# The start of the first layer reordered, and half PSUM banks for the projection steps beside attention

## The chip, the cores and the metric

The kernel runs on one core of a Trainium2 chip. The metric is device microseconds of one execution; three executions of the kernel before took 1530.9 to 1532.79 us, with a median of 1532.69 us. The engines are named as the profile names them: PE is TensorE (PEld its weight loads), DVE is VectorE, ACT is ScalarE, POOL is GpSimd, SP is SyncE, which issues every DMA of this kernel.

## The reference, cut to what matters

Two layers run one after the other on x (1024 tokens by 1024 features, float32). Each layer is

```
h = rms_norm(x, pre_norm)                       # rows of x times 1/rms, times a gain
proj = h @ w_in                                 # 1024 x 3072: q, k, v and gates of all heads
dq, dk = rotary(dq), rotary(dk)                 # differential attention, 6 heads x 2 maps
gq, gk = rotary(rms_norm(gq)), rotary(rms_norm(gk))   # grouped-query attention, 6 q / 2 kv heads
mk, mv = split(rms_norm(mem) @ w_mem_kv)        # cross attention into 256 memory tokens, 4 heads
o = softmax(q k^T) v  for each head, times silu(gate)
x = x + rms_norm(concat(o) @ w_out, post_norm)
```

Every product is done in split precision: an operand is kept as a rounded "hi" part and the rest as "lo", and three matmuls (hi by hi, hi by lo, lo by hi) stand for one.

## The kernel before, in words

**The planner.** No order is written out by hand. `Plan` runs all the work as small processes against a model of the engines. A process asks for an engine with a priority (a lower number goes first) and an assumed duration; when the model starts the job, its instructions are emitted. The order of emission is the program order of each engine and is fixed from then on. The tile framework under it then adds semaphores wherever two accesses to one tile have to be ordered, by that order. The planner knows only its own events and buffers, not these semaphores.

**The PSUM banks.** PSUM has eight banks. The planner's `Banks` (L145) hands out two tiles of two banks (`pp`, size 2) and four tiles of one bank of 512 columns (`ps`, size 1). `KINDS` (L83) gives each kind of use a priority, the most it may hold, and a size: `st` (projection steps beside attention) up to four, `mx` (row maxima of scores) four, `tr` (transposes) two, `pv` (probabilities times v) one, `s0` and `s1` (projection steps before attention) two each. All of these take from the same four `ps` tiles.

**A projection step** is one chunk of 256 columns of `w_in` for one tile of 128 tokens: 24 matmuls (L518) in four groups of six, a group for each quarter of the weights, all accumulating into 256 columns of a `ps` tile. So a step uses half of the bank that it holds. When its last group is done, `post` (L752) is started for it and `steps` (L807) goes straight on to the next step, which asks for its own slot. `post` empties the bank. For a gate chunk ACT reads it (tanh, L724) and then DVE reads it (L732). For q and k chunks ACT squares it (L676, only heads with a norm) and DVE does three rotary operations on it (L657 twice, once in place, and L659). For v parts ACT (L640) and DVE (L641) read it, and a plain copy is ACT's (L774). Then the slot is freed (`free_ps`). These reads have the priority `POST` of -1 on ACT and DVE; the matmuls of `st` steps have the last priority on PE.

**The stages of a layer.** First `steps` runs the chunks dq0 and dk0 (kinds s0 and s1), then dv0 and the memory's mk and mv. Then attention begins: the d items (12 score maps), later the g and m items. Beside it run the nine chunks of `REST` for eight token tiles, 72 steps of the kind `st`, four of the nine chunks being gates. After attention comes the output projection (L1444), whose tail also normalises and transposes x for the second layer.

**The first layer's begin** is `start_up` (L1752). One matmul group broadcasts the gain vector `pre_norm` over the partitions into a `pp` tile (L1786). Eight x tiles are loaded (five buffers, `XT`). `one(t)` takes each of them through `norm_T` (L489): ACT squares and sums (L491), POOL makes the inverse root (L454, L455), DVE multiplies by it and the gain (L501). Then `split_T` does, twice, four transposes on PE (L476), the hi copy on ACT (L480) and the lo difference on DVE (L481). The same DVE rotates the dq0 and dk0 steps meanwhile. `gm0` (L446) takes the greatest gain on DVE; the scale of v needs it. `weights` (L562) loads four pieces of each chunk through three `rt` buffers, splits them (L410, L411, L412) into eight `wt` slots and goes on to the next chunk when two pieces are ready. The rotary tables of the second kind are loaded and multiplied on POOL (L624, L626).

Of the kernel before, what the change touches and what calls it, by code (L numbers as in the profile page):

```python
# [12 lines left out]
F32 = mybir.dt.float32  # L13
# [9 lines left out]
P = 128  # L23
# [7 lines left out]
NC = 256  # L31
# [22 lines left out]
FIRST = ("dq0", "dk0", "dv0", "mk", "mv")  # L54
# [13 lines left out]
ALT0, ALT1, ALTM = (), (), ()  # L68
# [5 lines left out]
LAT = {"pe": 0.231, "act": 0.176, "dve": 0.165, "pool": 0.121, "hwdge": 0.65, "dma": 0.95}  # L74
DVE_FIX = 0.15
PV_N = 2
XT = 5
DMA_RATE = 300.0

CLOCK_WINDOW, CLOCK_LOW, CLOCK_HIGH = 3.41, 0.33, 0.85  # L80
SLACK = 0.8

KINDS = {'un': (0.5, 2, 2), 'z': (1, 2, 2), 's0': (2, 2, 1), 's1': (0, 2, 1), 'st': (1, 4, 1), 'pv': (1, 1, 1), 'tr': (-1, 2, 1), 'mx': (2, 4, 1), 'zh': (3, 2, 1)}  # L83


def raw(t):
# [3 lines left out]
class Event:  # L90
    def __init__(self, n=1):
        self.n = n
        self.waiters = []
# [51 lines left out]
class Banks:  # L145


    def __init__(self, tiles, kinds):
        self.free_tiles = tiles
        self.kinds = kinds  # L150
        self.held = {k: 0 for k in kinds}
        self.waiters = []
        self.seq = 0
# [6 lines left out]
    def grant(self, plan):  # L160
        rest = []
        while self.waiters:
            w = heapq.heappop(self.waiters)
            _, limit, size = self.kinds[w[3]]
            if self.held[w[3]] < limit and self.free_tiles[size]:
                self.held[w[3]] += 1
                plan.push(plan.t, w[2], (w[3], size, None, self.free_tiles[size].pop(0)))
            else:
                rest.append(w)
        for w in rest:  # L170
            heapq.heappush(self.waiters, w)

    def free(self, plan, slot):
        kind, size, _, t = slot
        self.free_tiles[size].append(t)
        self.held[kind] -= 1
        self.grant(plan)

# [109 lines left out]
def trunk(ctx, tc, t_in, t_out):  # L288
    nc = tc.nc
    act, dve, pool, pe = nc.scalar, nc.vector, nc.gpsimd, nc.tensor  # L290
    pl = Plan()
# [10 lines left out]
    big = ctx.enter_context(tc.tile_pool(name="big", bufs=16))  # L302
    psp = ctx.enter_context(tc.tile_pool(name="psum", bufs=1, space=PSUM))
    banks = Banks({2: [psp.tile([P, D], F32, name=f"pp{i}") for i in range(2)],
                   1: [psp.tile([P, 512], F32, name=f"ps{i}") for i in range(4)]}, KINDS)
    R = {"rt": Ring(RT_BUFS), "wt": Ring(W_SLOTS), "big": Ring(16)}

    def open_pool(name, bufs=1, side=None):
# [10 lines left out]
    def wait(ev):  # L319
        return "wait", ev  # L320
# [13 lines left out]
    def DVE(n, fn, prio=0, ops=1, fast=False, port=False):  # L334

        return use("dve", DVE_FIX * ops + n / (1900.0 if fast else 960.0), fn, prio, None, port)
# [126 lines left out]
    def free_ps(slot):  # L463
        banks.free(pl, slot)

    def split_T(src, hi, lo, halves=(0, 1), prio=0):

        done = Event(len(halves))

        def half(h):  # L470
            slot = yield take_ps("tr")
            ps = slot[3]

            def f():
                for j in range(4):
                    pe.transpose(out=ps[:, j * P:(j + 1) * P], in_=src(4 * h + j), identity=ident)  # L476

            yield PE(1024, f, prio)
            v = ps[:, 0:512].rearrange("p (b t) -> p b t", t=P)
            yield ACT(512, lambda: act.activation(hi[:, 4 * h:4 * h + 4, :], v, AF.Copy), prio, "p")  # L480
            yield DVE(512, lambda: dve.tensor_sub(out=lo[:, 4 * h:4 * h + 4, :], in0=v,  # L481
                                                  in1=raw(hi)[:, 4 * h:4 * h + 4, :]), prio)
            free_ps(slot)

        for h in halves:
            pl.spawn(half(h), done)
        yield wait(done)

    def norm_T(xt, gbc, hn, hi, lo, ev=None, alt=False):  # L489
        ss = small.tile([P, 1], F32, name="ss")  # L490
        yield ACT(1024, lambda: act.activation(hi.rearrange("p a b -> p (a b)"), xt, AF.Square, accum_out=ss))  # L491
        box = []
        yield from rstd_of(ss, 1, 1.0 / D, box, -2)
        if ev is not None:
            yield wait(ev)
            gbc = gbc[0]
        if alt:
            yield ACT(1024, lambda: act.activation(hn, xt, AF.Copy, scale=box[0][:, 0:1]))
            yield POOL(1024, lambda: pool.tensor_mul(out=hn, in0=hn, in1=gbc))
        else:  # L500
            yield DVE(1024, lambda: dve.scalar_tensor_tensor(out=hn, in0=xt, scalar=box[0][:, 0:1], in1=gbc,  # L501
                                                             op0=ALU.mult, op1=ALU.mult), port=ev is None)
        yield from split_T(lambda b: hn[:, b * P:(b + 1) * P], hi, lo)

    def new_big():
        return big.tile([P, S], F32R, name="big")
# [30 lines left out]
    def make_layer(l):  # L537
        L = Layer()
# [22 lines left out]

        def weights(chunks):  # L562
            for c in chunks:
                src = t_in["w_mem_kv"][l] if c in ("mk", "mv") else w_in
                vmax = None
                if c in VCOLS:
                    vmax = small.tile([P, 8], F32, name="gm")
                    pl.spawn(vscale(vmax, (lambda: mgm[0]) if c == "mv" else (lambda: L.gmx), L.W[c], sc, VKEY[c]))
                evs = []
                for j in range(4):  # L570
                    ev = Event()
                    pl.spawn(load_piece(src, j, CHUNKS[c], L.W[c], c, vmax, {FIRST[0]: -7, FIRST[1]: -5}.get(c, 0),
                                        L.rt.pop(0) if L.rt else None), ev)
                    evs.append(ev)
                if c != FIRST[0]:
                    yield wait(evs[1])
# [230 lines left out]
        def steps(chunks, kind, prio):  # L807

            todo = []
            for c in chunks:  # L810
                todo += [(c, t) for t in range(2 if c in ("mk", "mv") else NT)]
            yield wait(opened)
            for c, t in todo:
                n = 2 if c in ("mk", "mv") else NT
                if c in ("mk", "mv"):
                    yield wait(mem_ready[t])
                    hi, lo = mT[t]
                else:
                    yield wait(L.xT_ev[t])
                    hi, lo = L.xT[t]  # L820
                yield wait(L.W[c]["ev"][0])
                nat = None
                if c in scr:
                    ni = yield take("nat")
                    nat = (Q["pj"].tile([P, NC], F32, name="nat", bufs=NAT), ni)
                slot = yield take_ps(kind)
                ps = slot[3][:, 0:NC]
                yield from matmul_chunk(ps, hi, lo, L.W[c], t == n - 1, prio)
                if c == REST[-1]:
                    if t == 0:  # L830
                        rest_on.fire(pl)
                    for s in L.xT_slot[t]:
                        free("big", s)
                if c == "mv" and t == 1:
                    close_pool(pools["mp"])
                    open_attn()
                pl.spawn(post(c, t, slot, ps, nat), pend)
# [914 lines left out]
    def start_up():  # L1752
# [26 lines left out]
        def gain0():  # L1779

            slot = yield take_ps("z")
            ps = slot[3]

            def f():
                for h in range(2):
                    pe.matmul(ps[:, h * 512:(h + 1) * 512], lhsT=on[0:1, 0:P], rhs=grow[0:1, h * 512:(h + 1) * 512],  # L1786
                              start=True, stop=True)

            yield PE(8200, f)
            gbc.append(ps)  # L1790
            gain_ev.fire(pl)
            yield wait(L.xT_ev[1])
            yield DVE(1024, gm0, 2)
            for e in L.xT_ev:
                yield wait(e)
            free_ps(slot)

        def loads():
            g = dmas([(grow, t_in["pre_norm"][0:1], 4)], -10)
            yield "until", pl.t + 0.01  # L1800
            pl.spawn(load_x(0, evs[0], -9))
            pl.spawn(L.begin())
            yield wait(g)
            yield wait(on_ev)
            pl.spawn(gain0())
            pl.spawn(load_x(1, evs[1], -6))
            pl.spawn(dma(lin, t_in["lin_tab"], 128, -4))
            for t in range(2, NT):
                pl.spawn(load_x(t, evs[t], -3))
# [18 lines left out]
        def one(t):  # L1828
            yield wait(evs[t])
            b0 = yield take("big")  # L1830
            h = new_big()
            b1 = yield take("big")
            o = new_big()
            hi, lo = (x.rearrange("p (k t) -> p k t", t=P) for x in (h, o))
            L.xT[t] = (hi, lo)
            L.xT_slot[t] = (b0, b1)
            xt, i = xts[t]
            yield from norm_T(xt, gbc, xt, hi, lo, gain_ev, t in ALT0)
            free("xt", i)
            L.xT_ev[t].fire(pl)  # L1840

# [54 lines left out]
```

## Time and profile before

| | |
|---|---|
| median of three executions | 1532.69 us |
| the profiled execution's own time | 1529.82 us |
| its span | 1528.0 us |
| granted PE clock, mean over the span | 0.994 |
| PE busy | 1474.7 us (97%) |
| DVE, POOL, ACT busy | 1016.4, 907.6, 893.2 us |

The span runs from the first to the last instruction; the time has 1.8 us more around it. "Busy" is the time in which an engine had an instruction running. Matmuls overlap one another, so a busy PE can still be slower than its peak. In a row of the windows, the figure after an engine is its busy time in that stretch with the number of instructions, and PEclk is the granted share of the PE clock (0.50 is the lower of its two levels, 1.2 GHz instead of 2.4). In a row of the timeline the bracket says how long the engine had been idle before and what ended it.

### The profile page before, as it was taken

How to read it: one execution, taken by the hardware profiler on the slowest of the kernel's cores; microseconds unless marked ns; L12 is line 12 of the kernel's file. 1: busy time of each engine (PE TensorE's matmuls, PEld its weight loads, DVE VectorE, ACT ScalarE, POOL GpSimd, SP SyncE). 2: the span in 40 equal slices, each digit the busy share in tenths (PEclk: the TensorE clock that was granted, in tenths of full speed). 3: DMA queues.
4: the chain of work that ended last, by engine and by line, in shares of the span. 5: the costliest groups of instructions: out<-in, count | busy, mean ns of one | idle time of the engine just before them, and what ended most of it. 6: DMA issues, size and time to landing. Idle time of an engine off the chain costs nothing.

```text
span 1528.0 us, 39224 instructions
## 1 busy us (share of the span) xinstructions
PE 1474.7 (97%) x15920; PEld 1366.0 (89%) x15920; DVE 1016.4 (67%) x1886; ACT 893.2 (58%) x1429; POOL 907.6 (59%) x654
## 2 busy tenths in 40 slices
PE   6999999999999999999999999999999999999997
PEld 5999999999999988887889999999999998888886
DVE  6646676777864797844566386767877748887233
ACT  5232748677668486683333347578667756686511
POOL 5033848789778495571142348469897767685400
PEclk9999999999999999999999999999999999999999
DMA  6335322233232643215255433133342246422242
GB/s 221 107 115 153 85 81 81 85 105 99 77 94 80 170 123 92 72 57 183 97 170 159 124 103 104 42 102 94 102 118 60 65 121 192 113 68 71 95 138 97
DMA packets 166658, 164.75 MB, mean 108 GB/s; under 512 B 14924, under 2 KB 140588, under 8 KB 166477
## 3 DMA queue, kind: packets, MB, share of 16 engines
q1 hardware_dynamic: 166477, 162.25, 36.3%
q8 instruction: 125, 2.05, 0.6%
q14 instruction: 56, 0.46, 0.1%
HBM read 111.74 MB, written 50.09 MB: 106 GB/s over the span
## 4 chain that ended last, share of the span: by engine, by line
PE 81%; issue 6%; DVE 5%; DMA 3%; POOL 3%; ACT 1%; SPq 1%; POOLq 0%; DVEq 0%; ACTq 0%
PE ps L518 33%; PE pp L1444 9%; PE ps L1067 6%; PE pp L1077 6%; PE ps L529 4%; PE ps L531 4%; PE ps L530 4%; PE ps L1279 3%; PE ps L1280 2%; PE pp L1291 2%; PE pp L1292 2%; DVE mx L938 1%; PE ps L476 1%; PE ps L1444 1%; POOL el L901 1%
## 5 line engine op out<-in xcount | busy, mean ns | idle before, releaser
L901 POOL TENSOR_TENSOR el<-e,eh 128x1024 f16<-128x1024 f32 x254 | 563.4, 2231 | 169.2 <-ACT eh L898 161.1
L518 PE MATMUL ps<-wt,big 128*128 128x256 f32 x4608 | 642.4, 286 | 14.4 <-DVE sl L712 3.7
L518 PEld LDWEIGHTS ps<-wt,big 128*128 128x128 f32 x4608 | 605.9, 191 | 34.9 <-DVE sl L712 4.3
L938 DVE TENSOR_REDUCE mx<-ps 128x1 f32<-128x512 f32 (+1 forms) x608 | 404.2, 684 | 118.1 <-PE ps L1067 81.2
L894 ACT ACTIVATE e<-pp 128x1024 f32<-128x1024 f32 x304 | 308.9, 1023 | 99.5 <-PE pp L1077 52.2
L898 ACT ACTIVATE eh<-e 128x1024 f16<-128x1024 f32 x264 | 277.5, 1058 | 2.9
L529 PEld LDWEIGHTS <-eh 128*128 128x128 f16 x2144 | 194.8, 96 | 13.6 <-issue 9.0
L531 PEld LDWEIGHTS <-el 128*128 128x128 f16 x2144 | 196.5, 99 | 4.7 <-POOL el L901 4.2
L530 PEld LDWEIGHTS <-eh 128*128 128x128 f16 x2144 | 196.7, 97 | 0.9 <-issue 0.8
L412 POOL TENSOR_TENSOR wt<-rt,wt 128x512 fp32r<-128x512 f32 x84 | 122.4, 1469 | 123.8 <-ACT wt L410 87.0
L454 POOL TENSOR_SCALAR u<-ss 128x1 f32<-128x1 f32 (+3 forms) x95 | 23.6, 249 | 238.2 <-DVE ss L1585 96.2
L1067 PE MATMUL ps<-sdk,sdq 96*128 96x512 f32 x384 | 159.1, 414 | 0.8 <-DVE gs L732 0.8
L529 PE MATMUL ps<-vd,eh 128*128 128x65 f16 x1536 | 151.3, 193 | 0.0
L530 PE MATMUL ps<-vd,eh 128*128 128x64 f16 x1536 | 150.4, 194 | 0.0
L531 PE MATMUL ps<-vd,el 128*128 128x65 f16 x1536 | 149.9, 192 | 0.0
L1077 PE MATMUL pp<-sdq,sdk 98*128 98x256 f32 x768 | 125.3, 285 | 0.5 <-DMA sdq<-nl 0.5
L1077 PEld LDWEIGHTS pp<-sdq,sdk 98*128 98x128 f32 x768 | 113.6, 190 | 6.1 <-issue 0.8
L990 ACT ACTIVATE o<-ps 128x130 f32<-128x130 f32 (+1 forms) x160 | 45.9, 287 | 93.8 <-PE ps L531 93.1
L1291 PE MATMUL pp<-big 128*128 128x256 f32 x384 | 98.2, 287 | 0.0
L1292 PE MATMUL pp<-big 67*128 67x256 f32 x384 | 96.7, 284 | 1.3 <-DMA big<-nl 1.3
L455 POOL TENSOR_TENSOR r<-u,mhalf 128x1 f32<-128x1 f32 (+3 forms) x95 | 80.7, 849 | 7.9
L410 ACT ACTIVATE wt<-rt 128x512 fp32r<-128x512 f32 x124 | 75.1, 629 | 15.8 <-DMA rt<-in_w_in 8.5
(244 smaller groups left out, 2628.2 us busy)
## 6 DMA issues: line engine op xcount, KB each, us to landing
rt<-in_w_in SPq DMA_DIRECT2D x96, 128.0 KB
rt<-in_w_in SPq DMA_DIRECT2D x44, 256.0 KB
gt<-g_scr SPq DMA_DIRECT2D x32, 256.0 KB
rt<-in_w_out SPq DMA_DIRECT2D x32, 256.0 KB
sdq<-s_dqa SPq DMA_DIRECT2D x48, 128.0 KB
sdk<-s_dka SPq DMA_DIRECT2D x48, 128.0 KB
big<-s_gqa SPq DMA_DIRECT2D x24, 256.0 KB
big<-s_gqb SPq DMA_DIRECT2D x24, 256.0 KB
```

The source lines that it names most:

```text
L518: pe.matmul(ps, lhsT=x[:, kt, :], rhs=y[:, a, :], start=(kt == 0 and n == 0), stop=(kt == KT - 1 and n == 2))
L529: pe.matmul(o[:, 0:65], lhsT=eh, rhs=v[:, kt, 0:65], start=(kt == 0), stop=False, skip_group_check=True)
L530: pe.matmul(o[:, 0:64], lhsT=eh, rhs=v[:, kt, 66:130], start=False, stop=False, skip_group_check=True)
L531: pe.matmul(o[:, 0:65], lhsT=el, rhs=v[:, kt, 0:65], start=False, stop=(kt == n - 1), skip_group_check=True)
L894: yield ACT(1024, lambda: act.activation(e, ps, AF.Exp, scale=scale), 0, "p")
L898: yield either((ACT(1024, lambda: act.activation(eh, e, AF.Copy)), 0.0), (DVE(1024, lambda: dve.tensor_copy(out=eh, in_=e), 0, fast=True, ...
L901: (POOL(1024, lambda: pool.tensor_sub(out=el, in0=e, in1=eh)), 0.0))
L938: yield DVE(512, lambda: dve.tensor_reduce(out=out_ap, in_=src, axis=AX.X, op=ALU.max), MXP[0])
L1067: yield (512, lambda ps, n=n: pe.matmul(ps, lhsT=q()[0:96, i * P:(i + 1) * P], rhs=k()[0:96, n * 512:(n + 1) * 512], start=True, stop=True ...
L1077: pe.matmul(ps[:, a * 256:(a + 1) * 256], lhsT=k()[0:98, kt * P:(kt + 1) * P], rhs=q()[0:98, j * 256:(j + 1) * 256], start=True, stop=True)
L1291: pe.matmul(o, lhsT=ka()[:, ks], rhs=a()[:, qs], start=True, stop=False)
L1444: pe.matmul(z, lhsT=x[:, k, :], rhs=y, start=(k == KT_ORDER[0] and n == 0), stop=(k == KT_ORDER[-1] and n == 2))
```

## The change

Two groups of edits.

**Start of the first layer.** (1) The DVE multiply of x tile t now waits until tile t-2 is through its transposes and splits (`AHEAD` = 2, `prev`). (2) The transposes, hi copies and lo differences of x get the priority -2 in place of 0 on PE, ACT and DVE. (3) `weights` holds back the chunk dv0, and with it all later chunks, until x tile 5 is transposed (`X_GATE`). (4) The load of x tile 1 gets the priority -6.5 in place of -6, and the third and fourth piece of dq0 -6 in place of -7, so that x tile 1 can be issued ahead of those two. (5) `gm0` runs after all x tiles in place of after tile 1.

**Half banks.** The kind `st` gets the size 0. Where no half is free, a free `ps` tile is cut in two halves of 256 columns; a free half is always taken before a new tile is cut; when both halves are free they become one tile again. The limit stays at four, now four halves. The step's matmuls and reads address the half's 256 columns.

```diff
-KINDS = {..., 'st': (1, 4, 1), ...}
+KINDS = {..., 'st': (1, 4, 0), ...}
 def grant(self, plan):
...
             _, limit, size = self.kinds[w[3]]
+            if size == 0 and not self.free_tiles[0] and self.free_tiles[1]:
+                t = self.free_tiles[1].pop(0)
+                self.free_tiles[0] += [(t, 0), (t, 1)]
             if self.held[w[3]] < limit and self.free_tiles[size]:
...
 def free(self, plan, slot):
         kind, size, _, t = slot
         self.free_tiles[size].append(t)
+        if size == 0 and (t[0], 1 - t[1]) in self.free_tiles[0]:
+            self.free_tiles[0] = [x for x in self.free_tiles[0] if x[0] is not t[0]]
+            self.free_tiles[1].append(t[0])
...
 def norm_T(...):
+        if prev is not None:
+            yield wait(prev)
...
-        yield from split_T(lambda b: hn[:, b * P:(b + 1) * P], hi, lo)
+        yield from split_T(..., hi, lo, prio=0 if ev is None else -2)
 def weights(chunks):
             for c in chunks:
+                if l == 0 and c == FIRST[2]:
+                    yield wait(L.xT_ev[X_GATE])
...
-   {FIRST[0]: -7, FIRST[1]: -5}.get(c, 0)
+   {FIRST[0]: -7 + (j > 1), FIRST[1]: -5}.get(c, 0)
 def steps(chunks, kind, prio):
                 slot = yield take_ps(kind)
-                ps = slot[3][:, 0:NC]
+                t_ps, half = slot[3] if isinstance(slot[3], tuple) else (slot[3], 0)
+                ps = t_ps[:, half * NC:(half + 1) * NC]
 def gain0():
-            yield wait(L.xT_ev[1])
-            yield DVE(1024, gm0, 2)
             for e in L.xT_ev:
                 yield wait(e)
+            yield DVE(1024, gm0, 2)
...
-            pl.spawn(load_x(1, evs[1], -6))
+            pl.spawn(load_x(1, evs[1], -6.5))
...
-            yield from norm_T(xt, gbc, xt, hi, lo, gain_ev, t in ALT0)
+            yield from norm_T(xt, gbc, xt, hi, lo, gain_ev, t in ALT0, L.xT_ev[t - AHEAD] if t >= AHEAD else None)
```

## Rows read from the trace of the kernel before

**Rows 1.** The page, part 1: busy time, share of the span, instructions
```profile
PE 1474.7 (97%) x15920; PEld 1366.0 (89%) x15920; DVE 1016.4 (67%) x1886; ACT 893.2 (58%) x1429; POOL 907.6 (59%) x654
```
**Rows 2.** Windows over the two stretches with REST steps: busy us, PEclk, DMA share
```profile
115.00:526.00 411.00, 404.65 (x4810) 387.44 (x4809) 287.62 (x596) 259.33 (x415) 291.73 (x208) 1.00 0.35 99
865.00:1273.00 408.00, 401.88 (x4799) 384.75 (x4798) 286.30 (x596) 258.33 (x414) 290.79 (x206) 1.00 0.36 100
```
**Rows 3.** Windows of 4 us at the start: PE, PEld, DVE, ACT, POOL, PEclk
```profile
24.00:28.00 4.00, 3.56 (x31) 3.32 (x31) 3.96 (x9) 1.57 (x4) 1.43 (x3) 1.00 0.67 226
28.00:32.00 4.00, 1.09 (x6) 0.61 (x6) 4.00 (x6) 2.12 (x4) 3.39 (x8) 0.83 0.01 5
32.00:36.00 4.00, 1.77 (x7) 1.29 (x7) 4.00 (x7) 0.77 (x2) 0.00 (x0) 0.50 0.11 33
36.00:40.00 4.00, 4.00 (x21) 4.00 (x20) 1.22 (x3) 0.87 (x2) 0.00 (x0) 0.50 0.34 98
```
**Rows 4.** Timeline of the start: start us, duration us, engine, line, out<-in
```profile
10.42 1.05 ACT L491 ACTIVATE big<-xt 128x1024 fp32r<-128x1024 f32 x1
...
11.98 0.58 ACT L480 ACTIVATE big<-ps 128x512 fp32r<-128x512 f32 x1
...
13.70 0.68 DVE L481 TENSOR_TENSOR big<-ps,big 128x512 fp32r<-128x512 f32 x1
...
15.46 4.50 PE L518 MATMUL ps<-wt,big 128*128 128x256 f32 x30
...
27.32 1.42 POOL L624 TENSOR_TENSOR turnk<-turnk,gaink 128x256 f32<-128x256 f32 x2 [2.03 <-DMA turnk<-in_ax_tab]
...
30.76 0.19 POOL L454 TENSOR_SCALAR u<-ss 128x1 f32<-128x1 f32 x1
...
31.94 1.21 DVE L446 TENSOR_REDUCE gmx<-pp 128x1 f32<-128x1024 f32 x1
```
**Rows 5.** Groups by line and shape, 115 to 526 us: busy, mean ns, idle before
```profile
L518 PE MATMUL ps<-wt,big 128*128 128x256 f32 x1728 | 244.7, 285 | 5.5 <-DVE sl L712 2.0 <-DVE vg L641 1.6 <-ACT sh L711 1.5
...
L732 DVE SCALAR_TENSOR_TENSOR gs<-sq,ps 128x256 f32<-128x256 f32 x31 | 12.8, 414 | 22.4 <-ACT sq L724 15.6 <-ACT e L894 6.2 <-DMA g_scr<-gs 0.5
L724 ACT ACTIVATE sq<-ps 128x256 f32<-128x256 f32 x32 | 12.2, 382 | 38.8 <-PE ps L518 17.4 <-DVE mx L938 13.7 <-DVE gs L732 7.7
L659 DVE TENSOR_TENSOR nat<-ps,rb 128x128 f32<-128x128 f32 x32 | 9.3, 292 | 1.9
...
L657 DVE TENSOR_TENSOR rb<-ps,turnq 128x256 f32<-128x256 f32 x8 | 3.3, 409 | 0.0
...
L676 ACT ACTIVATE sq<-ps 128x256 f32<-128x256 f32 x8 | 3.1, 384 | 2.1 <-PE ps L518 2.1
...
L640 ACT ACTIVATE vg<-ps,vc 128x128 f16<-128x128 f32 x8 | 3.0, 369 | 7.8 <-PE ps L518 3.4 <-DVE nat L659 3.2 <-DVE wm L423 1.2
```
**Rows 6.** Line L640: what ended its idle time, then who waited for it
```profile
  DVE nat L659: 6.2, 4
...
  DVE rb L657: 2.2, 6
```
**Rows 7.** Timeline of one dk1 step's reads and the next step's first matmul
```profile
202.36 0.29 DVE L659 TENSOR_TENSOR nat<-ps,rb 128x128 f32<-128x128 f32 x1
...
202.75 0.37 ACT L640 ACTIVATE vg<-ps,vc 128x128 f16<-128x128 f32 x1 [1.65 <-DVE nat L659]
...
203.56 0.39 PE L518 MATMUL ps<-wt,big 128*128 128x256 f32 x1 [1.61 <-DVE vg L641]
```
**Rows 8.** Timeline of a gq0 step's reads beside the next step's matmuls
```profile
353.30 0.39 ACT L676 ACTIVATE sq<-ps 128x256 f32<-128x256 f32 x1 [0.57 <-PE ps L518]
353.34 2.31 PE L518 MATMUL ps<-wt,big 128*128 128x256 f32 x18
...
353.72 0.42 DVE L684 TENSOR_REDUCE ss<-sq 128x4 f32<-128x256 f32 x1 [0.54 <-ACT sq L676]
...
354.91 0.42 DVE L659 TENSOR_TENSOR nat<-ps,rb 128x256 f32<-128x256 f32 x1
```

More of the change, by code (lines that the diff above doesn't have):

```diff
@@ L76 @@
 PV_N = 2
-XT = 5
+X_GATE, XT, AHEAD = 5, 5, 2
 DMA_RATE = 300.0
@@ L81 @@
 SLACK = 0.8
-KINDS = {'un': (0.5, 2, 2), 'z': (1, 2, 2), 's0': (2, 2, 1), 's1': (0, 2, 1), 'st': (1, 4, 1), 'pv': (1, 1, 1), 'tr': (-1, 2, 1), 'mx': (2, 4, 1), 'zh': (3, 2, 1)}
+KINDS = {'un': (0.5, 2, 2), 'z': (1, 2, 2), 's0': (2, 2, 1), 's1': (0, 2, 1), 'st': (1, 4, 0), 'pv': (1, 1, 1), 'tr': (-1, 2, 1), 'mx': (2, 4, 1), 'zh': (3, 2, 1)}
 def raw(t):
@@ L304, in trunk @@
     banks = Banks({2: [psp.tile([P, D], F32, name=f"pp{i}") for i in range(2)],
-                   1: [psp.tile([P, 512], F32, name=f"ps{i}") for i in range(4)]}, KINDS)
+                   1: [psp.tile([P, 512], F32, name=f"ps{i}") for i in range(4)], 0: []}, KINDS)
     R = {"rt": Ring(RT_BUFS), "wt": Ring(W_SLOTS), "big": Ring(16)}
@@ L487, in split_T, with norm_T @@
         yield wait(done)
-    def norm_T(xt, gbc, hn, hi, lo, ev=None, alt=False):
+    def norm_T(xt, gbc, hn, hi, lo, ev=None, alt=False, prev=None):
         ss = small.tile([P, 1], F32, name="ss")
@@ L502, in norm_T @@
                                                              op0=ALU.mult, op1=ALU.mult), port=ev is None)
-        yield from split_T(lambda b: hn[:, b * P:(b + 1) * P], hi, lo)
+        yield from split_T(lambda b: hn[:, b * P:(b + 1) * P], hi, lo, prio=0 if ev is None else -2)
     def new_big():
@@ L571, in weights @@
                     ev = Event()
-                    pl.spawn(load_piece(src, j, CHUNKS[c], L.W[c], c, vmax, {FIRST[0]: -7, FIRST[1]: -5}.get(c, 0),
+                    pl.spawn(load_piece(src, j, CHUNKS[c], L.W[c], c, vmax, {FIRST[0]: -7 + (j > 1), FIRST[1]: -5}.get(c, 0),
                                         L.rt.pop(0) if L.rt else None), ev)
```

## The prediction

> **What bounds the kernel now.** I read the page's busy times first: PE is busy for 97% of the span and the next engine, DVE, for 67% [rows 1]. So the whole kernel lasts as long as PE's chain of matmuls plus what PE stands still, 1528.0 - 1474.7 = 53.3 us, and only two things can move the time: taking away standstill, or adding some. Then I looked at where the standstill lies, by windows. In the two stretches in which `REST` steps run beside attention it is 411 - 404.7 = 6.3 us and 408 - 401.9 = 6.1 us [rows 2]: little, in more than half of the kernel. At the start it is dense: between 24 and 36 us PE works 6.4 us of 12, and from 28 to 40 us the granted clock falls from 1.00 to 0.50, the lower of its levels, after PE has stood idle [rows 3]. The change touches these two places, so I price them one by one. The sums go against the profiled execution, 1529.8 us, which is 2.9 us below the median of the runs.
>
> **The start (edits 1 to 5).** Two losses can go.
>
> First, the first projection matmul runs at 15.46 us. It waits for the lo part of x tile 0's second half, which DVE makes at 13.70 (0.68 us) because ACT copies that half only at 11.98, after the square of x tile 1 (10.42, 1.05 us) [rows 4]. With the priority -2 the copy goes ahead of that square: 10.5 + 0.6 us for the copy, 0.7 for the difference, matmul at about 12.2. That is 3.3 us.
>
> Second, PE's gaps between 24 and 36 us are 0.44 + 2.91 + 2.23 = 5.6 us, and between 28 and 40 us it works 1.09 + 1.77 + 4.00 = 6.9 us, most at half clock, of which 3.4 us come back at the full one [rows 3]. DVE is full there (3.96, 4.00 and 4.00 of 4): it takes normalisations of several x tiles in a row, and `gm0`, 1.21 us at 31.94, before the differences for which PE waits. Behind that stands POOL: it waits 2.03 us for a rotary table, multiplies from 27.32 on, and only at 30.76 comes to the inverse root of a late x tile [rows 4]. `AHEAD` and the priorities put the differences first, and `gm0` leaves the stretch.
>
> The three together are 3.3 + 5.6 + 3.4 = 12.3 us. The DVE work itself doesn't shrink and POOL's order is only in part changed, so I take two thirds: 8 us. The bounds are 0 and 12.3 us. What these edits delay costs nothing that I can see: dv0's pieces are needed only after 16 steps of dq0 and dk0 (16 x 24 matmuls, some 0.12 us apart by the 2.31 us for 18 [rows 8]: 46 us of PE from 12 us on), while x tile 5 is done in the thirties even now; holding their four transfers back also takes them off SP's queue, in front of x tiles and tables. If that cover is gone (dv0 late), it is one chunk's load and split at about 58 us, a few us. The swap of x tile 1 with the last dq0 pieces moves a transfer by one place: nothing within the 8 us. What is late next is DVE.
>
> **Half banks: what they take away.** PE's waits for a free `ps` tile: the REST matmuls idle 5.5 us in the first layer, released by DVE and ACT reads that empty a bank [rows 5]. The second layer stands still as long [rows 2]. With halves the four `st` slots fit in two banks, so these waits go: 10 us for both layers.
>
> **Half banks: what they add.** A step's slot is asked for the moment the step before has ended, when that one still holds its half. The free half that `Banks` gives first is therefore, nearly always, the other half of the bank that ACT and DVE are just beginning to read. Now look at how the program treats two engines on one bank. A dk1 step has its bank read by DVE in columns 0 to 127 and by ACT in 128 to 255; nothing of the data ties the two. Yet ACT waits until DVE is through (202.36 + 0.29 = 202.65, ACT starts at 202.75 after 1.65 us idle) [rows 7]. It does so four times with 6.2 us idle, and the other way round DVE's first rotary operation waits six times for ACT's read [rows 6]. So accesses of different engines to one bank are put one after the other in program order, whatever the columns. No row shows a matmul into a bank whose other columns are being read, since no tile is used so now; I take it to be ordered in the same way.
>
> The Trainium skill, "PSUM — Partial Sum Buffer", section "PSUM bank collisions raise a hardware error", speaks against this edit: two engines may not touch one bank in the same partitions at once, a matmul's write and another engine's read of other columns included, so accesses have to be guarded by bank and not by address. For ACT and DVE the rows above agree (0.10 us from the end of the one to the start of the other); for PE's writes no row here shows it.
>
> The planner knows nothing of this order. It emits the first group of the next step about when the reads begin. In rows 8 ACT's square (353.30) comes before the next step's 18 matmuls (from 353.34), and the rotary operations, emitted with the reduction at 353.72, end at 355.33, all beside these matmuls. In one bank the first group would start after the square (0.4 us late), the rotary operations after that group (354.5), and the second group after them: 354.5 + 3 x 0.41 = 355.7 in place of 354.06, so PE stands 1.7 us, about all of that step's reading time.
>
> Reading time of a step on its bank, from rows 5: a gate 0.38 + 0.41 = 0.80 us; gq0 0.38 + 3 x 0.41 = 1.6; for the mixed chunks about 0.3 a read of 128 columns (0.29 on DVE, 0.37 for the slowest on ACT): dq1 seven reads 2.1, dk1 and gq1 five 1.5 each, dv1 three 0.9. Per layer that is 32 x 0.80 + 8 x (1.6 + 2.1 + 1.5 + 1.5 + 0.9) = 25.6 + 60.8 = 86 us, for two layers 173 us. What hides it is PE's other work that happens to lie between two groups: REST matmuls are 244.7 of 404.7 us of PE's busy time [rows 2, 5], so the other 40% is attention. If a read meets either by these shares, 60% of it becomes standstill: 104 us. Bounds: below, all reads fall on attention work, 0; above, none do, and each of some 2.4 runs of reads per step has a handover of 0.1 us [rows 7]: 173 + 144 x 2.4 x 0.1 = 208 us. The one pair followed above lies near the upper end, gates by their short reads nearer to the lower; I take 104. DVE and ACT, held back by a read that waits for a group (some 0.7 us), have slack (288 and 259 of 411 us [rows 2]).
>
> **Sum.** 1529.8 - 8 - 10 + 104 = 1616 us on the profile's execution; 2.9 more for the median of the runs: about 1619.
>
> **Rivals.**
> *A, faster: the halves hide.* The next step's groups come behind attention work, the reads are through by then, and the slot waits go. Then 1532.7 - 18 = 1515 us at best, 1521 with half the gain of the start. For it: 40% of PE's work is attention and `st` has PE's last priority, with more banks left for maxima. Against it: rows 8, where nothing lies between. It decides at 18 us of standstill, that is 18/144 = 0.125 us per step, a sixth of a gate's reads. The same time comes out if the matmuls are not ordered behind the reads, against rows 6.
> *B, no change.* The halves eat just the 18 us: 1533.
> *C, slower still: the order feeds on itself.* DVE, waiting for a group in a REST bank, also holds up the maxima in its queue, and PE then waits for their banks too: the upper bound of 208 us, 1532.7 - 18 + 208 = 1723.
> *D, the halves seldom share a bank* (a step's bank empty before the next asks, so that consecutive steps hardly meet): a fourth to a half of the cost, 26 to 52 us, 1541 to 1567. Against it: the slot is asked for at once.
>
> **How the numbers follow.** Forecast (1570 to 1680): 0.48. C, above 1680: 0.06. D, 1536 to 1570: 0.11. B: 0.06. A: 0.29. Faster and slower mean more than 0.2% (3 us), about what a measurement of this kernel tells from none: faster 0.29, same 0.06, slower 0.65. The likeliest case's own range is 1570 to 1680. To hold 8 in 10 the whole range has to take in A: 1514 to 1672, leaving out the best of A and the worst of the slow cases.
>
> **What would show it.** Start: the first L518 near 12 us, PEclk 1.00 between 28 and 40 us, REST beginning some 8 us earlier. Halves: the REST stretches grow from 411 and 408 us to about 460 each, PE's busy share in them falls from 98% to near 88%, and PE's waits at L518 name the reads L659, L641, L732, L676 and L724, 40 to 60 us per layer, while ACT and DVE lines name L518 more often. Waits at L518 that stay under 10 us per layer would make the forecast wrong and A right.

## The result and the profile after

The changed kernel takes 1631.88 us (median of four runs, 1630.4 to 1637.0) against 1532.68 us before: a ratio of 1.0656, 95% interval 1.0631 to 1.0682. It is slower by 99 us; the forecast was 1619 us. In the three later sets of runs the kernel before had medians of 1530.6 to 1533.1 us, so differences between runs of different sets carry some 2 us.

The page of the changed kernel, part 1 and the head of its groups (out<-in, count | busy us, mean ns | idle before, releaser); the projection matmuls are now line 528:

```profile
span 1629.0 us, 39270 instructions
...
PE 1516.0 (93%) x15920; PEld 1381.6 (85%) x15920; DVE 1017.5 (62%) x1891; ACT 897.8 (55%) x1433; POOL 886.5 (54%) x645
...
L528 PE MATMUL ps<-wt,big 128*128 128x256 f32 x4608 | 664.2, 290 | 75.6 <-DVE nat L671 37.2
```

The same 15920 matmuls [rows 1] now leave PE idle for 1629.0 - 1516.0 = 113 us in place of 53, and PE is "busy" 41 us longer without doing more. The idle time before the projection matmuls is 75.6 us, and DVE's last rotary read is what ends half of it.

The two stretches with `REST` steps run from the first such matmul to the last: 121.8 to 525.2 us and 870.8 to 1272.4 us before, 110.4 to 589.0 and 913.0 to 1392.9 us now. So they take 479 and 480 us in place of 403 and 402 us. The stretch from their end to the output projection is shorter (108 in place of 127 to 129 us), since more of the attention was done beside them (PE ran 5067 matmuls in the first stretch, 4810 before). Net, 54 and 59 us per layer are lost, and the start gained 11.4 us. Windows over the two stretches, columns as in [rows 2]:

```profile
110.00:589.00 479.00, 439.17 (x5067) 405.10 (x5066) 313.44 (x611) 276.69 (x432) 295.20 (x209) 0.99 0.30 84
913.00:1393.00 480.00, 440.18 (x5064) 406.00 (x5062) 312.42 (x611) 277.13 (x433) 294.41 (x208) 0.99 0.30 84
```

PE now stands still for 39.8 us in each, against 6.3 and 6.1 us [rows 2]. DVE, ACT and POOL are busy for a smaller share of the time too: no other engine became the bound. The waits of PE that lead its list over the whole span (line, releaser: us in total, times, longest):

```profile
PE ps L528 <- DVE nat L671: 37.2, 45, 2.3
PE ps L528 <- ACT vg L652: 7.0, 6, 1.2
PE ps L528 <- DVE gs L744: 7.0, 12, 0.9
PE ps L528 <- ACT sq L736: 6.8, 22, 0.5
...
PE ps L528 <- ACT sq L688: 5.2, 12, 1.4
```

These are the reads that the prediction named: L671 is L659 of before, L652 is L640, L744 is L732, L736 is L724, L688 is L676. With the shorter waits at L528 for such reads, further down the same list, they come to 71 us, 35 per layer. And this is one gq0 step's bank in the changed kernel, from the timeline, to be laid beside [rows 8]:

```profile
383.27 0.38 ACT L688 ACTIVATE sq<-ps 128x256 f32<-128x256 f32 x1 [1.33 <-DVE mx L951]
...
384.02 0.41 DVE L669 TENSOR_TENSOR rb<-ps,turnq 128x256 f32<-128x256 f32 x1
...
384.88 0.42 DVE L671 TENSOR_TENSOR nat<-ps,rb 128x256 f32<-128x256 f32 x1
...
385.45 0.94 PE L528 MATMUL ps<-wt,big 128*128 128x256 f32 x6 [1.33 <-DVE nat L671]
...
389.10 0.38 ACT L688 ACTIVATE sq<-ps 128x256 f32<-128x256 f32 x1 [0.39 <-PE ps L528]
...
389.53 0.98 PE L528 MATMUL ps<-wt,big 128*128 128x256 f32 x6 [0.29 <-ACT sq L688]
...
390.49 0.95 PE L528 MATMUL ps<-wt,big 128*128 128x256 f32 x6
...
391.48 0.42 DVE L669 TENSOR_TENSOR rb<-ps,turnq 128x256 f32<-128x256 f32 x1 [1.54 <-PE ps L528]
```

In [rows 8] 18 matmuls ran through all these reads. Here PE does nothing for 1.33 us and starts its group 0.15 us after the last read's end (384.88 + 0.42 = 385.30). The last four lines show the other half of the same order, one step later. That step's own matmuls were done when ACT read its half at 389.10; then PE ran two groups of the step after it into the other half, and DVE, idle for 1.54 us, could make its first rotary read only when they had ended (390.49 + 0.95 = 391.44).

At the start PE's gap and the low clock are gone, as forecast. The four windows of [rows 3], in the changed kernel:

```profile
24.00:28.00 4.00, 4.00 (x34) 3.82 (x34) 3.49 (x8) 1.62 (x4) 0.57 (x2) 1.00 0.32 117
28.00:32.00 4.00, 4.00 (x36) 4.00 (x35) 3.97 (x9) 2.15 (x5) 2.55 (x6) 1.00 0.23 66
32.00:36.00 4.00, 4.00 (x36) 4.00 (x35) 3.23 (x7) 0.87 (x2) 1.53 (x3) 1.00 0.34 98
36.00:40.00 4.00, 4.00 (x37) 4.00 (x36) 3.41 (x8) 1.28 (x3) 0.00 (x0) 1.00 0.88 273
```

PE is busy in all 16 us, 143 matmuls instead of 65 [rows 3], at the full clock. The first projection matmul comes at 11.15 us in place of 15.46. What stood before it, from the timeline before and after:

```profile
13.84 1.97 PE L476 MATMUL ps<-ident,xt 128*128 128x128 f32 x8 [3.17 <-DVE xt L501]
```

```profile
11.13 1.29 DVE L489 TENSOR_TENSOR big<-ps,big 128x512 fp32r<-128x512 f32 x2 [1.31 <-ACT big L488]
...
11.15 1.95 PE L528 MATMUL ps<-wt,big 128*128 128x256 f32 x6 [1.00 <-ACT big L488]
```

Before, PE stood for 3.17 us for DVE's multiply of x tile 1, whose transposes came ahead of the projection in PE's order. Now the projection comes first, and it waits for ACT's hi copy alone: the lo parts, made by DVE from 11.13 us on (L489), end after it has begun.

### The profile page after: what moved, and what is told of

Its sections match the earlier page's. It is cut to its first block, busy times and chain, and to the rows that moved or that the text cites. A ratio compares the mean times of both kernels' runs of the same rounds, so it can differ in the third digit from the quotient of the medians.

```text
span 1629.0 us, 39270 instructions
## 1 busy us (share of the span) xinstructions
PE 1516.0 (93%) x15920; PEld 1381.6 (85%) x15920; DVE 1017.5 (62%) x1891; ACT 897.8 (55%) x1433; POOL 886.5 (54%) x645
## 3 DMA queue, kind: packets, MB, share of 16 engines
q1 hardware_dynamic: 166477, 162.25, 34.2%
## 4 chain that ended last, share of the span: by engine, by line
PE 82%; DVE 8%; issue 3%; DMA 3%; ACT 3%; SPq 1%; POOL 1%; DVEq 0%; POOLq 0%; ACTq 0%
PE ps L528 35%; PE pp L1457 8%; PE pp L1090 5%; PE ps L1080 4%; PE ps L539 4%; PE ps L540 4%; PE ps L541 4%; PE ps L1292 3%; PE pp L1305 3%; PE pp L1304 3%; PE ps L1293 3%; DVE mx L951 1%; PE ps L484 1%; PE ps L1457 1%; PE ps L715 1%
## 5 line engine op out<-in xcount | busy, mean ns | idle before, releaser
L914 POOL TENSOR_TENSOR el<-e,eh 128x1024 f16<-128x1024 f32 x264 | 580.0, 2208 | 297.9 <-ACT eh L911 253.0
L528 PE MATMUL ps<-wt,big 128*128 128x256 f32 x4608 | 664.2, 290 | 75.6 <-DVE nat L671 37.2
L528 PEld LDWEIGHTS ps<-wt,big 128*128 128x128 f32 x4608 | 607.9, 192 | 122.8 <-DVE nat L671 23.6
L911 ACT ACTIVATE eh<-e 128x1024 f16<-128x1024 f32 x274 | 287.1, 1055 | 2.4
L539 PEld LDWEIGHTS <-eh 128*128 128x128 f16 x2208 | 203.1, 97 | 13.8 <-issue 8.5
L541 PEld LDWEIGHTS <-el 128*128 128x128 f16 x2208 | 204.8, 100 | 6.7 <-POOL el L914 6.7
L540 PEld LDWEIGHTS <-eh 128*128 128x128 f16 x2208 | 204.9, 98 | 0.9 <-issue 0.7
L420 POOL TENSOR_TENSOR wt<-rt,wt 128x512 fp32r<-128x512 f32 x75 | 106.4, 1428 | 143.5 <-ACT wt L418 112.4
```

The lines of the kernel that those rows point to most:

```text
L528: pe.matmul(ps, lhsT=x[:, kt, :], rhs=y[:, a, :], start=(kt == 0 and n == 0), stop=(kt == KT - 1 and n == 2))
L539: pe.matmul(o[:, 0:65], lhsT=eh, rhs=v[:, kt, 0:65], start=(kt == 0), stop=False, skip_group_check=True)
L540: pe.matmul(o[:, 0:64], lhsT=eh, rhs=v[:, kt, 66:130], start=False, stop=False, skip_group_check=True)
L541: pe.matmul(o[:, 0:65], lhsT=el, rhs=v[:, kt, 0:65], start=False, stop=(kt == n - 1), skip_group_check=True)
L911: yield either((ACT(1024, lambda: act.activation(eh, e, AF.Copy)), 0.0), (DVE(1024, lambda: dve.tensor_copy(out=eh, in_=e), 0, fast=True, ...
L914: (POOL(1024, lambda: pool.tensor_sub(out=el, in0=e, in1=eh)), 0.0))
```

## The experiments

Two neighbouring steps share when both write into the same bank. Such pairs can be counted from the program order of PE, in which each matmul names its `ps` tile (per layer, of 71 pairs of neighbouring `REST` steps; both layers have the same count but for the last row):

```
before                      3
start only                  3
two whole banks             1
never the neighbour's       1
other bank where possible  26
halves for gates only      27
halves for q, k, v only    39
changed kernel             63
one whole bank             32 and 29 (in turn: a step asks when the bank is empty)
```

**1. The start alone.** Half banks undone.

```diff
-KINDS = {..., 'st': (1, 4, 0), ...}
+KINDS = {..., 'st': (1, 4, 1), ...}
```

> The change with its half banks undone (st back to whole banks, up to four), the start's edits kept. If the matmuls of a step and the reads of the step before wait for one another in a shared bank, all of the loss goes and the start's gain stays: the changed kernel's REST begins 11.4 us earlier than before (110.4 against 121.8 us), so 1532.7 - 11 = 1521 us, REST stretches of some 403 us again, waits at the projection matmuls under 10 us per layer. If instead the new start throws the later order out (the rival), it stays near 1632 us.

Measured: 1519.27 us, ratio 0.9927 (0.9913 to 0.9940), faster than both kernels. `REST` begins at 110.7 us and lasts 402 us in the first layer, 401 in the second. So the start gains 11 us and none of the loss is its doing: that rival falls. Its page:

```profile
PE 1472.0 (97%) x15920; PEld 1364.6 (90%) x15920; DVE 1011.3 (67%) x1887; ACT 892.9 (59%) x1429; POOL 909.1 (60%) x653
```

**2. The half banks alone.** All five edits of the start undone, for instance

```diff
-                if l == 0 and c == FIRST[2]:
-                    yield wait(L.xT_ev[X_GATE])
...
-        yield from split_T(..., hi, lo, prio=0 if ev is None else -2)
+        yield from split_T(..., hi, lo)
...
```

> The half banks alone, the start as before. Bank order: the two parts add up, 1631.9 + 11 = 1643 us, REST stretches near 478 us each, first projection matmul at 15.5 us. Rival (the start's edits are to blame): near 1533 us.

Measured: 1643.67 us, ratio 1.0736 (1.0716 to 1.0756), as expected; `REST` lasts 480 us in each layer. The halves cost 113.1 us without the new start and 112.6 us with it: the two parts add up.

**3. The other bank where possible.** Halves out of two cut banks; one that isn't beside the step before is taken first.

```diff
-            if size == 0 and not self.free_tiles[0] and self.free_tiles[1]:
-                t = self.free_tiles[1].pop(0)
-                self.free_tiles[0] += [(t, 0), (t, 1)]
+            if size == 0:
+                far = [x for x in self.free_tiles[0] if x[0] is not self.last]
+                if not far and len(self.cut) < 2 and self.free_tiles[1]:
+                    t = self.free_tiles[1].pop(0)
+                    self.cut.append(t)
+                    far = [(t, 0), (t, 1)]
+                    self.free_tiles[0] += far
+                self.free_tiles[0] = far + [x for x in self.free_tiles[0] if x[0] is self.last]
...
```

> The whole change, but a step takes a half in another bank than the step before did, out of two cut banks (A0, B0, A1, B1 and so on). As many halves and as few banks as in the change, only neighbours no longer share. Bank order between neighbouring steps: the reads of a step are over 1.8 us after its end on average, a step lasts some 5.6 us, so nearly nothing meets: 1517 to 1530 us, waits at the projection matmuls under 15 us per layer. Rival (halves as such, or the planner's order with more banks left for maxima, cost the time): stays above 1600 us.

Measured: 1572.71 us, ratio 1.0276 (1.0262 to 1.0290): 53 us above the start alone, neither expectation. The count tells why: 26 pairs per layer still shared. (By the planner's rules a bank whose two halves have come free goes back to the maxima, so that often only the half beside the neighbour is left; this was not followed up.) That is 53.4/52 = 1.03 us for each sharing pair, against 112.6/126 = 0.89 us in the changed kernel. But not all of it is sharing: PE also waits 13.6 us for DVE's `nm` (L933), 0.9 us in the start alone, and these waits name no bank of a projection step. Here too DVE's last rotary read (L681 in this kernel, whose projection matmuls are L538) leads PE's waits:

```profile
PE ps L538 <- DVE nat L681: 20.4, 27, 1.4
```

**4. Two whole banks.**

```diff
-KINDS = {..., 'st': (1, 4, 0), ...}
+KINDS = {..., 'st': (1, 2, 1), ...}
```

> The start's edits, and whole banks for the projection steps but two at most, so that the maxima have as many banks as with halves. Bank order: no bank is shared, 1517 to 1530 us. Rival (the planner's order with two banks for st and more for the maxima is worse by itself): above 1600 us; a part of it would show as a time between.

Measured: 1522.43 us, ratio 0.9941 (0.9924 to 0.9959). The maxima had as many banks as with halves, so the rival that a plan with more banks for them is worse by itself falls as far as this plan shows it. It also bears on what the halves were to take away, the waits for a free bank. In the start alone the three of them that the prediction read (DVE's `sl` and `vg`, ACT's `sh`) are 3.4, 3.2 and 3.0 us; with two whole banks 1.3 us are left of them, but waits for other reads rose at the same line:

```profile
PE ps L528 <- DVE nat L671: 2.3, 4, 0.7
...
PE ps L528 <- DVE sl L724: 1.3, 2, 0.7
```

All waits for a bank at L528 fall from some 11 to some 6 us, and the kernel is no faster for it (1522.4 against 1519.3 us).

**5. Never the neighbour's.** As 3, but a step waits if only a half beside its neighbour's is free.

```diff
-            if self.held[w[3]] < limit and self.free_tiles[size]:
+            if self.held[w[3]] < limit and (self.free_tiles[size] if size else far):
```

> As the run before that took another bank than the neighbour's, but a step now waits in the planner if only a half beside its neighbour's is free: in program order 1 of 71 neighbouring pairs per layer shares a bank (63 in the change, 26 in the run before). Bank order between neighbours: 1515 to 1528 us, and the 53 us that the run before still lost were its 26 pairs. Rival (halves as such, or program order with halves, cost time apart from neighbours): 1560 us or more.

Measured: 1540.03 us, ratio 1.0076 (1.0051 to 1.0102); the runs spread from 1536 to 1549 us. Of the 53 us that 3 lost, 33 are gone with the 50 shared pairs. The standstill of PE inside the two `REST` stretches is down to that of the start alone: 5.1 and 4.8 us, against 16.6 and 16.7 in run 3 and 5.7 in the start alone. The window over the first:

```profile
110.00:527.00 417.00, 411.89 (x4926) 392.39 (x4925) 295.09 (x598) 270.89 (x424) 298.49 (x212) 1.00 0.35 96
```

The other 21 us over the start alone were not expected. They come with more standstill outside these stretches (47 us in place of 32), led by waits for the probabilities' low part, which POOL or DVE makes:

```profile
PE ps L551 <- POOL el L924: 9.8, 9, 2.0
PE ps L551 <- POOL elm L924: 5.3, 4, 2.0
...
PE ps L551 <- DVE elm L923: 3.3, 2, 1.7
```

Such waits are some 4 us in the start alone. So the planner drew another order of the attention, with its price; what in it leads to these waits was not looked for further.

**6 and 7. Halves for a part of the chunks.** A second kind `sf` with whole banks for the others.

```diff
-KINDS = {..., 'st': (1, 4, 0), ...}
+KINDS = {..., 'st': (1, 4, 0), 'sf': (1, 4, 1), ...}
...
-                slot = yield take_ps(kind)
+                slot = yield take_ps(kind if kind != "st" or c[1] == "g" else "sf")   # run 6
+                slot = yield take_ps(kind if kind != "st" or c[1] != "g" else "sf")   # run 7
```

> Start's edits; halves for the four gate chunks alone, whole banks for the other five: 27 of 71 pairs per layer share a bank. If a pair costs in proportion to its reads (0.80 us for a gate, 60 to 70% of it met): 54 x 0.80 x 0.65 = 28 us over the start alone, 1547 us. If every pair costs the same (113 us over 126 pairs, 0.89 us each): 48 us, 1567 us. If sharing is not the cause: as in the start alone, 1519 us, or as in the change.

Measured: 1562.64 us, ratio 1.0198 (1.0169 to 1.0228), runs from 1552.6 to 1566.0 us: near what the same price for every pair gives.

> Start's edits; halves for the five q, k and v chunks alone, whole banks for the gates: 39 of 71 pairs per layer share a bank. In proportion to the reads (1.52 us on average, 60 to 70% met): 78 x 1.52 x 0.65 = 77 us over the start alone, 1596 us. The same for every pair (0.89 us): 69 us, 1588 us. Together with the gates' run the two costs should add up to about the 113 us of the change.

Measured: 1603.90 us, ratio 1.0478 (1.0462 to 1.0495), above both expectations.

Over the start alone that is 43 us for 54 pairs of gates (0.80 us each, all of their reading time) and 85 us for 78 pairs of q, k and v (1.08 us each, 71% of theirs). They add up to 128 us, 15 more than the 113 of the change. So the cost follows the sharing, but these totals don't price the reads. Run 6's trace:

```profile
PE ps L541 <- POOL el L914: 10.1, 11, 2.0
PE ps L528 <- DVE gs L744: 9.6, 18, 0.9
PE ps L528 <- ACT sq L736: 5.6, 18, 0.5
PE ps L541 <- POOL elm L914: 4.8, 2, 2.7
```

Only the two lines at L528 are waits for gate reads, 15.2 us, a third of the 43 us that 54 gates are read for; the other two are the waits of run 5 again. PE's standstill inside the `REST` stretches, which holds the waits for shared banks, is 11.3 and 10.9 us in run 6 and 27.9 and 29.1 in run 7, against 5.7 in the start alone: 0.20 us for a pair of gates and 0.58 for one of q, k and v, a quarter and some 40% of their reads. What the rest of the 128 us is, in each run, was not followed.

**8. One whole bank, known to the planner.**

```diff
-KINDS = {..., 'st': (1, 4, 0), ...}
+KINDS = {..., 'st': (1, 1, 1), ...}
```

> Start's edits; projection steps beside attention get whole banks, but one step at a time: the next step's matmuls come only after the reads of the step before, as in a shared bank, only the planner knows it and can put attention work into the gap. If the loss comes from an order that the planner didn't see, this costs clearly less than the halves, though it gives less room: 1525 to 1580 us. If waiting for the reads as such costs the time, seen or not: 1630 us or more (1.83 us from a step's end to its last read less 0.55 us to the next step's first matmul, 144 times, would be 184 us).

Measured: 1616.48 us, ratio 1.0555 (1.0533 to 1.0577): above the first of its two expectations and below the second, nearly as slow as the change. The windows over its two `REST` stretches, and over those of the start alone:

```profile
111.00:577.00 466.00, 432.30 (x4989) 403.53 (x4988) 307.70 (x612) 275.03 (x430) 296.34 (x207) 0.98 0.31 87
909.00:1366.00 457.00, 422.76 (x4935) 395.55 (x4934) 305.30 (x608) 269.78 (x425) 295.19 (x207) 0.99 0.32 88
```

```profile
111.00:513.00 402.00, 396.25 (x4746) 379.64 (x4746) 282.13 (x586) 255.37 (x407) 289.19 (x205) 1.00 0.35 98
857.00:1258.00 401.00, 395.27 (x4748) 378.50 (x4748) 284.46 (x587) 255.88 (x408) 288.74 (x205) 1.00 0.35 98
```

PE stands still for 33.7 and 34.2 us in place of 5.8 and 5.7, although the planner, by its assumed durations, knew of the wait. But it stands for other things than in the change. The waits that lead the first stretch:

```profile
PE ps L528 <- DVE nat L671: 6.3, 4, 2.9
PE ps L715 <- POOL nat L705: 5.5, 6, 1.6
PE ps L1292 <- DMA big<-s_gqa: 4.9, 1, 4.9
```

A projection step still waits for reads (L528), but less than in the change (23 us over the whole span in place of 71); attention's own matmuls (L715, L1292), waiting for POOL and a DMA, take as much. That fits a planner that fills the gap with attention work which isn't ready, but only the waits are shown. So knowing the order did not save the time here: one step at a time costs 97 us over the start alone. It doesn't show that the hidden order plays no part in the change, since this run also puts more in a row than the halves do (all 24 matmuls of a step come behind all reads of the step before). My theory, that an order unseen by the planner is what makes the loss, found no support.

**9 to 11. The parts of the start.** On the kernel before: edit 2 alone; edits 1, 2 and 5; edits 3 and 4.

```diff
 run 9
-        yield from split_T(..., hi, lo)
+        yield from split_T(..., hi, lo, prio=0 if ev is None else -2)
 run 10 as run 9, and
+        if prev is not None:
+            yield wait(prev)
...
-            yield wait(L.xT_ev[1])
-            yield DVE(1024, gm0, 2)
             for e in L.xT_ev:
                 yield wait(e)
+            yield DVE(1024, gm0, 2)
...
 run 11
+                if l == 0 and c == FIRST[2]:
+                    yield wait(L.xT_ev[X_GATE])
...
-   {FIRST[0]: -7, FIRST[1]: -5}.get(c, 0)
+   {FIRST[0]: -7 + (j > 1), FIRST[1]: -5}.get(c, 0)
...
-            pl.spawn(load_x(1, evs[1], -6))
+            pl.spawn(load_x(1, evs[1], -6.5))
```

> The kernel before with edit 2 alone: priority -2 for the transposes, copies and differences of x. By the prediction's first term the first projection matmul comes at about 12 us in place of 15.5 and that is worth 3.3 us; if the differences also go ahead of the normalisations at 28 to 36 us, part of the 9 us there goes too: 1522 to 1529 us. If the normalisations taken in a row were the cause of the gap there, the clock still falls to half and it is 1527 to 1531 us.

> Edits 1, 2 and 5 (order on DVE, ACT and PE), without 3 and 4 (dv0's loads held back, x tile 1 ahead of two dq0 pieces). If the start's 11 us come from the order on DVE, this has nearly all of them: 1518 to 1523 us. If they come from SP's queue, where a dv0 transfer that waits for a buffer stands before x tiles and tables, less than half: 1525 to 1531 us.

> Edits 3 and 4 alone (the loads), the order of x on the engines as before. If the order on DVE is what counts: 1527 to 1531 us, half clock still between 31 and 41 us. If SP's queue is: 1519 to 1524 us, and POOL no longer waits 2 us for the rotary table.

Measured: 1522.74 us (ratio 0.9931, 0.9913 to 0.9950), 1534.29 us (1.0015, 1.0000 to 1.0031) and 1524.35 us (0.9947, 0.9928 to 0.9966). The first is as expected and at the better end. The second is a miss. The third misses its second range by 0.4 us, and the sign that went with that range came out: POOL no longer waits for the rotary table, which it multiplies from 24.97 us on (27.32 before). The beginning of `REST` in the first layer tells more than the totals: 112.4, 112.5 and 113.8 us, against 121.8 before and 110.7 with all five edits. Each group brings 8 to 9.4 us by itself, and together 11.1: they take away the same gap. The window in which the kernel before was nearly idle, for run 9 and run 11:

```profile
28.00:32.00 4.00, 3.98 (x34) 3.98 (x35) 3.89 (x8) 2.10 (x5) 2.60 (x6) 1.00 0.58 188
```

```profile
28.00:32.00 4.00, 2.33 (x14) 2.10 (x15) 3.96 (x7) 1.05 (x4) 1.09 (x4) 0.86 0.11 33
```

The priority of the splits alone fills it; the loads alone do half and shorten the low clock, and the first projection matmul still comes late, at 14.5 us (10.4 in run 9). Run 10 gained as much by the time `REST` began and lost it again in the second layer: `REST` takes 410 us there (402 before), the stretch from its end to the output projection 142 (127), that projection 112 (121). No edit touches these places; the planner's order there differs (5 pairs of the second layer share a bank in place of 3).

## Why the prediction was right, point by point

- *What bounds the kernel*: right. PE's standstill was all there was to gain or lose. What fell short is how standstill turns into time. PE's idle time rose by 113.0 - 43.4 = 70 us from the start alone (span 1515.4, PE busy 1472.0 us) to the changed kernel, 68 of them inside the `REST` stretches, and the time by 113. The rest is 44 us of "busy" time, on which the sum had nothing. The mean granted clock is 0.986 in place of 0.996, which makes 2 x 0.014 x 1629 = 46 us at half clock in place of 2 x 0.004 x 1515 = 12 us, and 34 us more at half clock are some 17 us lost (an estimate); some 20 of the 46 us lie behind the `REST` stretches, where the granted clock is 0.95. Another 18 us would be the loss of overlap at each restart: a matmul takes 0.285 us but its follower starts after 0.119 [rows 5, 8], 0.17 us for each of some 106 more stops of PE; that is worked out, and no run shows it apart. Some 9 us stay open.
- *The start, 8 us*: right in kind, too small. It is 11 us, near the upper bound of 12.3: PE's gap and the low clock went wholly, and the first projection matmul came at 11.2 us, where 12.2 was worked out. What PE waited for there in the trace was misread: not the lo part of tile 0 but the multiply of x tile 1 (3.17 us), and the changed kernel starts without the lo part. The priorities alone bring most of it (run 9), so neither `AHEAD` nor `gm0` was needed for that. That the loads by themselves bring nearly as much (run 11) had no price in the sum; the prediction names SP's queue only in passing.
- *Slot waits, -10 us*: no gain is shown. In run 4 about half of these waits go and the time doesn't fall.
- *The shared bank, 104 us*: right in its mechanism, down to the lines that PE waits for, with 63 of 71 pairs sharing ("nearly always"). That a matmul into the other half is put in order with the reads, which no row of before showed, is shown by the gq0 step above, in both directions. That the size came out too, 113 us, is in part luck. The 104 us were to be standstill, and the standstill is 68 us; the 44 us of busy time make up for it. Its own signs say the same: the waits at L528 are 35 us per layer where 40 to 60 were forecast, PE's share in the stretches is 91.7% and not near 88%, and the stretches are 479 and 480 us long and not 460, of which the shorter attention behind each gives back some 20 us.
- *The share of reading time that becomes standstill, 60%*: 68 of 173 us is 40%. That gates lie at the lower end holds for the standstill (a quarter of their reads in run 6, some 40% for the longer chunks in run 7), though not for the totals.
- *"The planner knows nothing of this order"*: true of the kernel, but run 8, where it knows of a like wait, loses 97 us over the start alone.
- *Rival A* would have needed under 0.125 us of standstill per step; 68/144 = 0.47 us were measured. (By its own terms its time with half the gain of the start is 1519 and not 1521 us.) *C* did not come about: PE's waits for DVE's maxima are under 4 us in all. *D* falls with 63 of 71 pairs sharing. The sum missed by 13 us: 10 from the slot waits that brought nothing and 9 from the shared bank, less 3 from the start and some 2 by which the kernel before was faster in the runs that gave these terms.

## What to carry to other kernels

A half-filled PSUM bank was not free room while another engine read the other half. The accesses came in order by bank (or by tile: a `ps` tile is one whole bank, so no run tells the two apart), and giving the rest to the next matmul group laid the reads of one group end to end with the matmuls of the next. Count in program order how often neighbours share a bank before giving the halves out, and look at the reads between; a planner that knew of such a wait lost nearly as much (run 8). And where an order comes out of a greedy planner, judge an edit by the stretch that it touches as well as by the total: run 5 lost 21 us and run 10 some 12 us with hardly a bank shared.

## What the runs showed that was not expected

A stall of PE cost more than its idle time: 70 us more of idle came with 44 us more of busy for the same 15920 matmuls. And two edits that by themselves let `REST` begin 9 and 8 us earlier (the splits' priority, the order of the loads) bring 11 together.
